# Decayed attention of a two-block network on one Trainium2 core: six gate groups go between the heads, the norm factors reach the features in one fp32r product, the sums of squares go into column groups

## The chip, the cores and the metric

The kernel runs on one core of a Trainium2 chip. Five engines of the core work side by side, each through its own list of instructions in order: TensorE (PE in the rows; PEld is its weight load), VectorE (DVE), ScalarE (ACT), GpSimd (POOL) and SyncE (SP), which issues the loads. Products go to PSUM; VectorE and ScalarE read it from there, GpSimd doesn't. The metric is the device time of one execution in microseconds.

## The reference, cut to what matters

The network is a first block (two layers of attention and a mixture of experts) and a second block of four layers: Fox (decayed attention), GLA, GDN, and Fox again, each followed by a SwiGLU. There are 256 tokens of 1024 features; the second block puts 16 meta tokens ahead of them. The change lies in the Fox layers alone:

```
def fox_mixer(h, w_in, b_f, q_gain, k_gain, w_out):
    proj = h @ w_in
    q, k, v, gate, f = jnp.split(proj, [D_MODEL, 2 * D_MODEL, 3 * D_MODEL, 4 * D_MODEL], axis=-1)
    q = rmsnorm(q.reshape(B, L, H, Dh), q_gain) * (Dh ** -0.5)
    k = rmsnorm(k.reshape(B, L, H, Dh), k_gain)
    v = v.reshape(B, L, H, Dh)
    log_f = jax.nn.log_sigmoid((f + b_f).astype(jnp.float32))
    c = jnp.cumsum(log_f, axis=1).transpose(0, 2, 1)
    ...
    # per query: softmax over earlier keys of q.k + c_query - c_key, times v
    o = o * jax.nn.sigmoid(gate)
    return (o @ w_out).astype(h.dtype)
```

H is 16 heads of Dh = 64 features. The queries of the meta tokens see meta keys only.

## The kernel before

Activations stand with features on the partitions: 8 tiles of 128 features by T2 = 272 tokens (256 in the outputs of the last layer). A projection (`proj`, L1832) makes one tile of 128 output features at a time, a group: 24 products of 128x128 weights with 128x272 activations into one PSUM tile `ps_mm`. There are 24 for 8 tiles of inputs, since weights and activations are split into a high and a low part (`wh`, `wl`; `hh`, `hl`) of the type fp32r, and high by high, high by low and low by high are summed. The pieces of the weights come through the class `Stream`: SyncE loads them ahead into `wraw`, ScalarE copies the high part (L312), VectorE subtracts for the low part (L322); of a plan whose mode is "both", GpSimd subtracts for every second piece.

The code is written in the order in which each engine's list is to stand; there is no scheduler. After a group `step` issues small work: what `later` has put into `due` for that tick, and up to `bg` = 2 pieces of `after_group` (one less when something was due). `flush` issues all that is left.

A Fox layer goes: 8 groups of queries, a small projection for log f, 8 groups of keys, 8 of values, 8 of gates, `flush`, the attention, and the output projection. Small work stands between the groups:

- `qk_evac`: ScalarE copies a group (L1977) and squares it (L1979); TensorE then sums the squares of each head by a product with `headsel` (L1974, 16 rows of output), one product after each group, 16 in a layer.
- `root`, `factor`: from these sums the factors of the norm, one row per head, on VectorE and ScalarE.
- `unit`/`one`: TensorE spreads the factors over the features by a product with `hb` (L2026, fp32, 16 rows deep), once per tile of queries or keys, 16 in a layer; VectorE multiplies (L2030) into `qS` and `kS`, with two `ps_t` tiles in turn.
- `v_tr`: TensorE transposes a tile of values (L2048, L2049), ScalarE copies it.
- `meta_scores`, `meta_soft`, `meta_norm`, `meta_trans`: the attention of the 16 meta tokens, all heads at once, in the first Fox layer alone (`lo` = 0). They come between gate groups.

The attention is a software pipeline over 16 heads (`pipe`, L701): in turn i it issues `trans` of head i-4 (TensorE transposes the weights P, L2158 and L2160; ScalarE and VectorE copy them, L2161, L2164, L2166), `scores` of head i (L2132 to L2136), `soft` of i-1 (VectorE's maxima L2142, ScalarE's exponentials L2144), `norm` of i-2 (L2149, L2151 on VectorE and GpSimd) and, every second turn, `pv` of a pair of heads (L2175 to L2182). The last five turns have no scores.

Of the kernel before, what the change touches and what calls it, by code (L numbers as in the profile page):

```python
# [26 lines left out]
# columns of the key tiles of the first mixer: first block, meta tokens, padding, both blocks  # L27
BIG = 4096.0
CAP = 128
YROWS = 14 * 128      # rows of the experts whose results go through memory; a row of zeros follows  # L30
# [4 lines left out]
# ------------------------------------------------------------------ host layout  # L35
# [95 lines left out]
def gla_masks():  # L131
# [5 lines left out]
    out[:, 0, :] = out[:, 4:].sum(1)        # the blocks of 16 and more together  # L137
# [42 lines left out]
def fm(t):  # L180
    """[tokens, 1024] to [128, 8, tokens]"""
    return np.ascontiguousarray(t.T.reshape(8, 128, -1).transpose(1, 0, 2))


def pack_rows(w, k0, n0):
    """chunks of k0 k-tiles by n0 columns: [chunk, 128, k0 * n0]"""
# [83 lines left out]
# ------------------------------------------------------------------ program  # L270

class Stream:
    """the weights, in pieces of up to 1024 columns, in the order of use: loads run ahead, and so do the splits"""
# [12 lines left out]
    def lend(self, tiles, name):  # L286
        """more room, each tile for one piece, from the first piece of that name on"""
        self.spare.extend(tiles)
        self.taker = next(i for i, p in enumerate(self.plan) if p[0][0][0] == name)

    def hold(self, name=None):
        """no loads beyond the first piece of that name, or no such bound"""
# [32 lines left out]
    def _fetch(self):  # L325
        """loads as far ahead as there are buffers that nothing to come reads"""
# [10 lines left out]
    def _reach(self, n):  # L337
        """the end of the next n pieces, not counting raw ones between them"""
# [26 lines left out]
class Net:  # L365
# [3 lines left out]
    def __init__(self, tc, aps, voff, coff, stack, phases):  # L369
# [12 lines left out]
        self.after_group = deque()      # background work for the tensor engine  # L382
        self.due = deque()              # work that waits for the evacuation of a group
        self.tick = 0
        self.bg = 2                     # pieces of background work after a group
# [4 lines left out]
    # ---- small helpers  # L390
# [40 lines left out]
    def step(self):  # L431
        """after the products of a group of a projection"""
# [8 lines left out]
    # ---- set-up  # L441
# [25 lines left out]
    # ================================================== first block  # L467
# [9 lines left out]
    def block1_alloc(self):  # L477
# [3 lines left out]
        # columns 0 .. 31 are for the router, the last two hold the conditions  # L481
# [17 lines left out]
    def mod_work(self, l, g):  # L499
        """closures: one part of the modulation of layer l, 2048 columns"""  # L500
# [2652 lines left out]
```

## Time and profile before

| what | value |
|---|---|
| three runs | 2823.67, 2824.31, 2826.16 us (median 2824.31) |
| span of the profiled execution | 2826.5 us |
| TensorE busy | 2699.9 us, 96% |
| VectorE busy | 1882.4 us, 67% |
| ScalarE busy | 1503.5 us, 53% |
| GpSimd busy | 509.4 us, 18% |
| mean granted TensorE clock | 0.977 |

The profile gives no other time of its own execution than the span, from the first to the last instruction; it is 0.3 us above the slowest of the three runs. Busy shares are averages over stages with different limits. The first Fox layer lies at about 1254 to 1444 us of the span, the second at about 2460 to 2635 us.

### The profile page before, as it was taken

Reading aid. Unit: us, or ns where it says so; the run is one execution under the profiler, and the core shown is the slowest. Engines: PE = TensorE matmul, PEld = TensorE weight load, DVE = VectorE, ACT = ScalarE, POOL = GpSimd, SP = SyncE. Lnnn points to the kernel's source line nnn. Section 1 sums busy time; section 2 is a strip of 40 time slices with the busy share of each in tenths; the row PEclk is TensorE's granted clock in tenths of the full one; section 3 lists DMA queues with packets and bytes.
Section 4 is the critical chain, followed back from the end, with each engine's and each line's share of the span. In section 5 each row is a group of like instructions: output and inputs, shape, how many; then the busy total and the mean of one; then the engine's idle time right before and its main releaser. Section 6 shows DMA issues by size and latency. Waiting matters only on the chain.

```text
span 2826.5 us, 46780 instructions
## 1 busy us (share of the span) xinstructions
PE 2699.9 (96%) x17848; PEld 2349.1 (83%) x17848; DVE 1882.4 (67%) x3094; ACT 1503.5 (53%) x2438; POOL 509.4 (18%) x482
## 2 busy tenths in 40 slices
PE   7999899999798999979899999999999999999999
PEld 4755678887576788868799998999889999987999
DVE  3257667778546889966766666665785666566664
ACT  2255467777445777754544444544553444445543
POOL 0111343231411100030210044101440200302100
PEclk9999999999799999989999999999999999999999
DMA  7544158999374699943245453455531354531554
GB/s 287 165 149 142 52 198 314 335 321 331 117 244 170 243 337 353 358 146 122 68 150 172 153 177 98 157 166 162 170 104 55 102 173 152 185 123 61 179 173 142
DMA packets 155450, 516.31 MB, mean 183 GB/s; under 512 B 22362, under 2 KB 25658, under 8 KB 155084
## 3 DMA queue, kind: packets, MB, share of 16 engines
q1 hardware_dynamic: 151440, 500.23, 52.3%
q10 hardware_dynamic: 2628, 8.83, 0.8%
q0 software_dynamic: 1152, 4.19, 0.4%
q8 instruction: 143, 2.34, 0.3%
q14 instruction: 87, 0.71, 0.1%
HBM read 504.42 MB, written 8.76 MB: 182 GB/s over the span
## 4 chain that ended last, share of the span: by engine, by line
PE 47%; DVE 6%; ACT 2%; issue 1%; POOL 1%; DMA 0%; ACTq 0%; DVEq 0%; POOLq 0%
PE ps_mm L1807 41%; DVE f L2551 1%; PE ps_t L2026 1%; DVE wl L322 1%; PE ps_s L1974 1%; DVE st L2142 1%; DVE B L2164 0%; ACT B L2144 0%; PE ps_t L2831 0%; PE ps_s L2840 0%; POOL acc L1761 0%; PE ps_mm L1860 0%; PE ps_s L2300 0%; PE ps_s L2175 0%; PE ps_o L1793 0%
## 5 line engine op out<-in xcount | busy, mean ns | idle before, releaser
L1807 PE MATMUL ps_mm<-B,wh 128*128 128x272 f32 (+1 forms) x6656 | 1271.1, 291 | 8.4 <-ACT B L1750 4.1
L322 DVE TENSOR_TENSOR wl<-wraw,wh 128x1024 fp32r<-128x1024 f32 (+2 forms) x853 | 997.8, 1196 | 128.9 <-ACT wh L312 120.1
L1807 PEld LDWEIGHTS ps_mm<-B,wh 128*128 128x128 f32 x6656 | 1049.7, 190 | 33.1 <-issue 20.2
L312 ACT ACTIVATE wh<-wraw 128x1024 fp32r<-128x1024 f32 (+2 forms) x882 | 881.7, 1013 | 197.8 <-PE ps_mm L1807 103.4
L1807 PE MATMUL ps_mm<-B,wl 128*128 128x272 f32 (+1 forms) x3328 | 962.9, 289 | 2.4 <-DVE wl L322 2.3
L1807 PEld LDWEIGHTS ps_mm<-B,wl 128*128 128x128 f32 x3328 | 631.2, 190 | 3.1 <-DVE wl L322 3.1
L1807 PE MATMUL ps_mm<-W,wh 128*128 128x512 f32 (+1 forms) x736 | 206.0, 367 | 5.2 <-ACT W L554 3.1
L1761 POOL TENSOR_TENSOR acc<-acc,sq 128x272 f32<-128x272 f32 (+1 forms) x49 | 78.8, 1608 | 641.5 <-issue 444.4
L1807 PEld LDWEIGHTS ps_mm<-W,wh 128*128 128x128 f32 x736 | 130.9, 192 | 39.3 <-ACT W L803 4.2
L1267 PE MATMUL ps_mm<-wh,W 128*128 128x512 f32 x512 | 162.1, 398 | 0.0
L1267 PE MATMUL ps_mm<-wh,XX 128*128 128x512 f32 x512 | 161.2, 396 | 0.0
L1807 PE MATMUL ps_mm<-W,wl 128*128 128x512 f32 (+1 forms) x368 | 132.0, 359 | 0.4 <-DVE wl L322 0.4
L1892 ACT ACTIVATE B<-f 128x272 fp32r<-128x272 f32 (+1 forms) x88 | 37.7, 428 | 171.1 <-DVE f L1890 171.1
L1267 PEld LDWEIGHTS ps_mm<-wh,W 128*128 128x128 f32 x512 | 96.9, 189 | 21.8
L1267 PEld LDWEIGHTS ps_mm<-wh,XX 128*128 128x128 f32 x512 | 96.7, 189 | 21.5
L1888 DVE TENSOR_TENSOR f<-ps_mm,R 128x272 f32<-128x272 f32 (+1 forms) x88 | 38.4, 437 | 112.8 <-PE ps_mm L1807 112.8
L1205 POOL TENSOR_SCALAR PP<-moec,rt_slm 128x128 fp32r<-128x128 f32 x60 | 80.7, 1362 | 177.3 <-PE ps_t L1233 177.3
L1299 PE MATMUL ps_s<-wl,ah 128*128 128x512 f32 x256 | 102.2, 399 | 5.4 <-PEq L1487 3.2
L1267 PE MATMUL ps_mm<-wl,W 128*128 128x512 f32 x256 | 103.7, 405 | 2.2 <-DVE wl L322 2.2
L1267 PE MATMUL ps_mm<-wl,XX 128*128 128x512 f32 x256 | 103.6, 405 | 1.3 <-ACT wh L312 0.9
L1299 PE MATMUL ps_s<-wh,al 128*128 128x512 f32 x256 | 101.1, 395 | 0.2 <-DVE al L1288 0.2
L1299 PE MATMUL ps_s<-wh,ah 128*128 128x512 f32 x256 | 101.2, 395 | 0.0
(727 smaller groups left out, 3653.1 us busy)
## 6 DMA issues: line engine op xcount, KB each, us to landing
wraw<-in_moe SPq DMA_DIRECT2D x376, 512.0 KB, 6.1
wraw<-in_wgu SPq DMA_DIRECT2D x176, 512.0 KB, 4.6
wraw<-in_w_mod SPq DMA_DIRECT2D x80, 512.0 KB, 4.7
wraw<-in_fox_in SPq DMA_DIRECT2D x64, 512.0 KB, 4.8
wraw<-in_wdn SPq DMA_DIRECT2D x64, 384.0 KB, 3.1
wraw<-in_wdn SPq DMA_DIRECT2D x64, 320.0 KB, 3.5
wraw<-in_gdn_in SPq DMA_DIRECT2D x32, 512.0 KB, 3.6
wraw<-in_gla_in SPq DMA_DIRECT2D x24, 512.0 KB, 3.9
```

The source lines that it names most:

```text
L312: nc.scalar.activation(wh[:, :n], t[:, :n], AF.Copy)
L322: (nc.gpsimd if pool or mode == "both" and key[1] else nc.vector).tensor_tensor(wl[:, :n], t[:, :n], wh[:, :n], op=OP.subtract)
L1205: eng.tensor_scalar(PP[:, b, i * 128:(i + 1) * 128], iota_n, u3(slm)[:, b, 2 * pair + i:2 * pair + i + 1], None, op0=OP.is_equal)
L1267: nc.tensor.matmul(ps, A[:, k, sl], B[:, d], start=n_ == 0, stop=n_ == 23)
L1299: nc.tensor.matmul(acc[c], A[:, sl], B[:, d], start=first and n_ == 0, stop=last and n_ == 11)
L1761: eng.tensor_add(self.acc[:, :n], self.acc[:, :n], sq[:, :n])
L1807: nc.tensor.matmul(ps[:, :n], A[:, k, :], B[:, :n], start=start and i == 0, stop=stop and i == tot - 1)
L1888: nc.vector.tensor_mul(t2[:, :n], pu[:, :n], self.R[:, :n])
L1892: nc.scalar.activation(ah[q][:, r, :n], av[:, :n], AF.Copy)
L1974: nc.tensor.matmul(sums[which][:16, :T2], hs[:, m, :], sq, start=m == 0, stop=m == 7)
L2026: nc.tensor.matmul(pb[:, :T2], hb[:, m * 128:(m + 1) * 128], rr[which], start=True, stop=True)
L2142: V.tensor_reduce(s[:, i:i + 1], p[:, c0:c0 + n], axis=AX.X, op=OP.max, negate=True)
```

## The change

Three things change in the Fox layers; elsewhere only comments go and line numbers shift.

1. **Sums of squares.** `add` waits for four groups and then issues four products that write to rows 0, 32, 64 and 96 of one PSUM tile, where each group had its own product before. `root` adds the four parts: six small operations on VectorE before the square root, where there were two.
2. **Factors.** They are split into a high and a low part of type fp32r in one tile `zf` (rows 0 to 15 and 32 to 47). The product in `one` is then an fp32r product 48 rows deep, not an fp32 product 16 rows deep. `hb` moves into four tiles of other buffers and is filled by 12 operations on GpSimd. During the groups of values `bg` is 3.
3. **Gates.** Only two groups of gates stand ahead of the attention. The other six are cut into halves of 12 products, and the pipeline issues one half at the end of each of its first 12 turns. Four of the eight low parts of the gates' weights go to GpSimd (mode "both"). The sigmoid becomes a tanh on ScalarE and an added 1 on GpSimd, and the values carry the factor 0.5. The copy of the meta weights (L2166) goes from VectorE to GpSimd. `yh` and `yl` get buffers of their own, since the groups of gates still read `hh` and `hl`. `meta_scores` and what follows it are issued after the two groups, with nothing of a projection between them.

```diff
+        p[12:] = [x[:3] + ("both",) + x[4:] for x in p[12:]]
...
+        sums, rr, fr = {}, {}, {}
...
+        hb = [self.t(nm, [128, 276], F32R, bufs=2)[:48, :256] for nm in ("f2", "f3") for _ in range(2)]
...
-            nc.gpsimd.tensor_copy(hb.rearrange("p (h f) -> p h f", h=16), sel[:16, :, None].to_broadcast([16, 16, 64]))
+            for i in range(4):
+                nc.gpsimd.tensor_scalar(hb[i], self.ones[:48, 0:1].to_broadcast([48, 256]), 0.0, None, op0=OP.mult)
+                for r in (0, 32):
+                    nc.gpsimd.tensor_scalar(hb[i][r:r + 16].rearrange("p (h f) -> p h f", h=4),
+                                            sel[r:r + 16, 4 * i:4 * i + 4, None].to_broadcast([16, 4, 64]), 1.0, None, op0=OP.mult)
 
         def qk_evac(which, raw):
-            def add(m, sq):
-                if m == 0:
+            sqs = []
+
+            def add(m):
+                if m == 3:
                     sums[which] = self.ps("s")
-                nc.tensor.matmul(sums[which][:16, :T2], hs[:, m, :], sq, start=m == 0, stop=m == 7)
+                for i in range(4):
+                    nc.tensor.matmul(sums[which][32 * i:32 * i + 16, :T2], hs[:, m - 3 + i, :], sqs[m - 3 + i], start=m == 3, stop=m == 7)
...
-                self.later(lambda: add(m, sq), 1)
+                sqs.append(sq)
+                if m % 4 == 3:
+                    self.later(lambda: add(m), 1)
...
         def root(which):
             R = self.R[:16]
-            t = rr[which] = self.u("zr", [16, T2], F32, bufs=2)
-            V.tensor_mul(t, R, R)
-            V.tensor_mul(t, sums[which][:16, :T2], t)
+            p = sums[which]
+            t = rr[which] = self.u("zr", [16, T2], F32)
+            V.tensor_copy(t, p[0:16, :T2])
+            for i in range(1, 4):
+                V.tensor_add(t, t, p[32 * i:32 * i + 16, :T2])
+            for _ in range(2):
+                V.tensor_mul(t, t, R)
             nc.scalar.activation(t, t, AF.Sqrt, bias=self.eps6[:16], scale=1.0 / 64)
 
         def factor(which):
             t = rr[which]
             V.reciprocal(t, t)
             V.scalar_tensor_tensor(t, t, 0.125 if which == "q" else 1.0, self.R[:16], op0=OP.mult, op1=OP.mult)
+            f = fr[which] = self.u("zf", [48, T2], F32R)
+            nc.gpsimd.tensor_scalar(f, self.ones[:48, 0:1].to_broadcast([48, T2]), 0.0, None, op0=OP.mult)
+            nc.scalar.activation(f[0:16], t, AF.Copy)
+            V.tensor_sub(f[32:48], t, f[0:16])
...
-                nc.tensor.matmul(pb[:, :T2], hb[:, m * 128:(m + 1) * 128], rr[which], start=True, stop=True)
+                nc.tensor.matmul(pb[:, :T2], hb[m // 2][:, m % 2 * 128:m % 2 * 128 + 128], fr[which], start=True, stop=True)
...
+            nc.scalar.activation(Vt[:, :, c], p[:, :256].rearrange("p (b c) -> p b c", b=2), AF.Copy, scale=0.5)
...
+        bg, self.bg = self.bg, 3
         self.proj(key, 8, T2, v_evac, c0=8)
-        sg = kraw
+        self.bg = bg
...
-            V.tensor_mul(g, ps[:, :T2], self.R)
-            nc.scalar.activation(sg[:, m, :], g, AF.Sigmoid)
-            if m == 2:
-                self.after_group.append(scratch)
-                if not lo:
-                    self.after_group.append(meta_scores)
-
-        # the attention's scratch, in the place of the raw queries and values
+            V.tensor_mul(g, ps[:, :T2], R)
+
+            nc.scalar.activation(g, g, AF.Tanh, scale=0.5)
+            nc.gpsimd.tensor_scalar(sg[:, m, :], g, 1.0, None, op0=OP.add)
...
-        self.proj(key, 8, T2, g_evac, c0=12)
+
+        self.after_group.append(scratch)
+        if not lo:
+            self.after_group.append(meta_scores)
+        self.proj(key, 2, T2, g_evac, c0=12)
         self.flush()
-        yh, yl = self.B(F32R), self.B(F32R)
-        blocks = ((16, 16, 0, 144), (144, 0, 160, 272))      # queries, keys, columns: 0 .. 143; 256 .. 271, 0 .. 255
+        hh, hl = self.hh, self.hl
+        yh, yl = (self.u(nm, [128, 8, T2], F32R) for nm in ("yh", "yl"))
+
+        def gates_left():
+            for m in range(2, 8):
+                wh, wl = (w.rearrange("p (k c) -> p k c", k=8) for w in self.ws.next((key, 12 + m // 2), m % 2))
+                p = self.ps("mm")
+                for k in (0, 4):
+                    self.group(p, wh[:, k:k + 4], wl[:, k:k + 4], hh, hl, 4, T2, k0=k, start=k == 0, stop=k == 4)
+                    if k == 0:
+                        yield
+                self.step()
+                g_evac(m, p)
+                yield
+
+        left = gates_left()
...
-                V.tensor_copy(PT[h % 4][0:16, 0:16], mm["t"][:, h * 16:(h + 1) * 16])
+                nc.gpsimd.tensor_copy(PT[h % 4][0:16, 0:16], mm["t"][:, h * 16:(h + 1) * 16])
...
-        self.pipe(16, (4, trans), (0, scores), (1, soft), (2, norm), (5, pv))
+        self.pipe(16, (4, trans), (0, scores), (1, soft), (2, norm), (5, pv), (0, lambda h: next(left, None)))
```

On TensorE, in the groups of queries of the first Fox layer, this stood before (`ps_s` takes the sums, `sq` are the squares):

```order
L1974 MATMUL ps_s_11704<-sq_11668,csts 16x272
L1974 MATMUL ps_s_11704<-sq_11671,csts 16x272
L1807 MATMUL ps_mm_11717<-B_11486,wh_11574 128x272
...
L1807 MATMUL ps_mm_11717<-B_11486,wl_11619 128x272
L1974 MATMUL ps_s_11704<-sq_11709,csts 16x272
L1807 MATMUL ps_mm_11752<-B_11486,wh_11617 128x272
...
L1974 MATMUL ps_s_11704<-sq_11744,csts 16x272
```

and now:

```order
L1807 MATMUL ps_mm_11727<-B_11486,wl_11622 128x272
L1983 MATMUL ps_s_11752<-sq_11679,csts 16x272
L1983 MATMUL ps_s_11752<-sq_11682,csts 16x272
L1983 MATMUL ps_s_11752<-sq_11685,csts 16x272
L1983 MATMUL ps_s_11752<-sq_11719,csts 16x272
L1807 MATMUL ps_mm_11766<-B_11486,wh_11620 128x272
...
L1807 MATMUL ps_mm_11766<-B_11486,wl_11689 128x272
L1807 MATMUL ps_mm_11800<-B_11486,wh_11687 128x272
```

The product that stood after every group is gone; after every fourth group four products into one `ps_s` stand in a row.

On TensorE, at the beginning of the attention of the first Fox layer, this stood before (L2119 is `meta_trans`, L1807 a gate group, L2132 to L2136 the scores of a head, L2158 the transposes):

```order
L2119 MATMUL ps_t_12856<-csts,mm_p_12781 16x16 x16
L1807 MATMUL ps_mm_12884<-B_11486,wh_12748 128x272
...
L1807 MATMUL ps_mm_12884<-B_11486,wl_12789 128x272
L2132 MATMUL ps_mm_12914<-kS_1316_11534,B_11532 128x144
L2132 MATMUL ps_mm_12914<-kS_1316_11534,B_11532 128x272
L2136 MATMUL ps_mm_12914<-causal,identb 128x16
L2132 MATMUL ps_mm_12920<-kS_1317_11535,B_11533 128x144
...
L2158 MATMUL ps_t_12959<-csts,B_11538 128x128 x3
```

and now (L2112 is `meta_scores`, L2138 `meta_trans`, L2170 to L2174 the scores):

```order
L2112 MATMUL ps_s_12690<-kS_1317_11535,B_11533 16x16
L2138 MATMUL ps_t_12721<-csts,mm_p_12714 16x16 x16
L2170 MATMUL ps_mm_12742<-kS_1316_11534,B_11532 128x144
L2170 MATMUL ps_mm_12742<-kS_1316_11534,B_11532 128x272
L2174 MATMUL ps_mm_12742<-causal,identb 128x16
L1807 MATMUL ps_mm_12754<-B_11486,wh_12556 128x272
...
L1807 MATMUL ps_mm_12754<-B_11486,wl_12609 128x272
L2170 MATMUL ps_mm_12767<-kS_1317_11535,B_11533 128x144
...
L1807 MATMUL ps_mm_12754<-B_11486,wh_12556 128x272
```

Half a group of 12 products now stands behind the scores of each of the first 12 heads, and `meta_trans` follows `meta_scores` directly.

On GpSimd, in the same stretch, this stood before (L2080 to L2084 clear scratch, L2151 normalises the weights of a head):

```order
L1968 COPY hb_11539<-csts 16x1024
L2081 MEMSET B_11530 128x512
L2084 MEMSET B_11538 128x16 x4
L2151 TENSOR_SCALAR B_11538<-B_11538,st_12926 128x272
L2151 TENSOR_SCALAR B_11538<-B_11538,st_12937 128x272
L2151 TENSOR_SCALAR B_11538<-B_11538,st_12951 128x272
```

and now (L2088 adds the 1 to a gate, L2189 is the old L2151, L322 the low part of a piece of weights, L2204 the copy of meta weights):

```order
L2088 TENSOR_SCALAR B_11531<-f_1408_12708 128x272
L2088 TENSOR_SCALAR B_11531<-f_1420_12790 128x272
L2189 TENSOR_SCALAR B_11538<-B_11538,st_12773 128x272
L322 TENSOR_TENSOR wl_12810<-wraw_12362,wh_12748 128x1024
L2189 TENSOR_SCALAR B_11538<-B_11538,st_12800 128x272
L2088 TENSOR_SCALAR B_11531<-f_1426_12853 128x272
L2204 COPY B_11530<-PmT_12738 16x16
L2189 TENSOR_SCALAR B_11538<-B_11538,st_12833 128x272
L2204 COPY B_11530<-PmT_12738 16x16
```

The normalisation of a head now stands in one queue with gates, weights and copies.

## Rows read from the trace of the kernel before

**Rows 1.** The page's first line, and the chain of waits by engine.
```profile
span 2826.5 us, 46780 instructions
...
PE 47%; DVE 6%; ACT 2%; issue 1%; POOL 1%; DMA 0%; ACTq 0%; DVEq 0%; POOLq 0%
```

**Rows 2.** Chain of waits, queries of the first Fox layer: start, us, what.
```profile
1258.10 1.48 PE ps_s L1974 x6
1259.57 3.21 PE ps_mm L1807 x24
1262.79 0.56 PE ps_s L1974 x2
```

**Rows 3.** The same chain, values and gates of the first Fox layer.
```profile
1347.49 0.22 PE ps_s L2048 x2
1347.70 0.11 PE ps_s L2049
1347.81 0.65 PE ps_t L2026 x2
1348.46 3.22 PE ps_mm L1807 x24
1351.69 1.11 PE ps_t L2026 x4
```

**Rows 4.** Windows, both attentions: busy PE, PEld, DVE, ACT, POOL; then TensorE clock, DMA.
```profile
1373.95:1418.29 44.34, 36.20 (x274) 24.83 (x272) 33.99 (x127) 25.17 (x89) 15.90 (x16) 1.00 0.02 5
2569.70:2611.16 41.46, 37.00 (x274) 25.48 (x272) 30.10 (x111) 25.30 (x89) 15.90 (x16) 0.96 0.04 13
```

**Rows 5.** Timeline of TensorE, router of the first block: start, us, what.
```profile
318.56 1.07 PE L1034 MATMUL ps_o<-W,wr 128*32 128x512 f32 x8
319.56 0.73 PE L1807 MATMUL ps_mm<-W,wh 128*128 128x512 f32 x2
```

**Rows 6.** Timeline of VectorE, and windows of tile mm_p (PE, PEld, DVE, ACT), meta attention.
```profile
1361.41 0.41 DVE L2102 TENSOR_REDUCE mm_mx<-ps_s 16x16 f32<-16x256 f32 x1
1366.16 0.24 DVE L2112 RECIPROCAL mm_s<-mm_s 16x16 f32<-16x16 f32 x1
...
1361.00:1374.00 13.00, 0.55 (x16) 0.44 (x16) 1.23 (x3) 0.42 (x1) 1.00 0.56 186
```

**Rows 7.** VectorE's groups, 1225 to 1475 us: count, busy us, mean ns, idle.
```profile
L322 DVE TENSOR_TENSOR wl<-wraw,wh 128x1024 fp32r<-128x1024 f32 (+1 forms) x51 | 61.5, 1211 | 13.2 <-ACT wh L312 10.4 <-DMA wraw<-in_fox_in 2.7
...
L2030 DVE SCALAR_TENSOR_TENSOR kS<-B,vecs,ps_t 64x256 f32<-64x256 f32 (+1 forms) x32 | 10.1, 353 | 7.7 <-PE ps_t L2026 7.6
...
L2166 DVE COPY B<-PmT 16x16 f32<-16x16 f32 x16 | 3.9, 242 | 0.5
...
L2055 DVE TENSOR_TENSOR B<-ps_mm,R 128x272 f32<-128x272 f32 x8 | 3.5, 442 | 0.1
```

**Rows 8.** Timeline of TensorE, first attention.
```profile
1383.02 0.41 PE L2132 MATMUL ps_mm<-kS,B 128*128 128x144 f32 x2
...
1383.99 0.90 PE L2175 MATMUL ps_s<-B,B 128*64 128x272 f32 x8
...
1385.25 0.55 PE L2158 MATMUL ps_t<-csts,B 128*128 128x128 f32 x3
...
1385.74 0.41 PE L2132 MATMUL ps_mm<-kS,B 128*128 128x144 f32 x2
...
1405.85 0.41 PE L2132 MATMUL ps_mm<-kS,B 128*128 128x144 f32 x2
```

**Rows 9.** Timeline of VectorE and GpSimd, first attention.
```profile
1380.52 0.16 DVE L2166 COPY B<-PmT 16x16 f32<-16x16 f32 x1
...
1381.52 1.06 POOL L2151 TENSOR_SCALAR B<-B,st 128x272 f32<-128x272 f32 x1 [1.36 <-DVE st L2149]
...
1382.27 0.34 DVE L2166 COPY B<-PmT 16x16 f32<-16x16 f32 x1
```

**Rows 10.** GpSimd's groups, whole span: count, busy us, mean ns, idle.
```profile
L322 POOL TENSOR_TENSOR wl<-wraw,wh 128x1024 fp32r<-128x1024 f32 x29 | 70.5, 2433 | 103.9 <-ACT wh L312 85.8 <-PE ps_t L2624 6.9 <-issue 6.2
```

More of the change, by code (lines that the diff above doesn't have):

```diff
@@ L1953, in fox @@
         vraw = self.B()
-        sums, rr = {}, {}
+        sums, rr, fr = {}, {}, {}
+        hb = [self.t(nm, [128, 276], F32R, bufs=2)[:48, :256] for nm in ("f2", "f3") for _ in range(2)]
         hs = self.cst("headsel").rearrange("p (m h) -> p m h", m=8)
         sel = self.cst("sel")
-        hb = self.u("hb", [16, 1024], F32)
         half = [slice(0, 64), slice(64, 128)]
@@ L2049, in v_tr @@
             nc.tensor.transpose(p[:48, 256:384], vraw[:, m, 224:272], self.ident)
-            nc.scalar.activation(Vt[:, :, c], p[:, :256].rearrange("p (b c) -> p b c", b=2), AF.Copy)
-            nc.scalar.activation(Vx[0:16, c], p[0:16, 128:256], AF.Copy)
-            nc.scalar.activation(Vx[32:48, c], p[32:48, 256:384], AF.Copy)
+            nc.scalar.activation(Vt[:, :, c], p[:, :256].rearrange("p (b c) -> p b c", b=2), AF.Copy, scale=0.5)
+            nc.scalar.activation(Vx[0:16, c], p[0:16, 128:256], AF.Copy, scale=0.5)
+            nc.scalar.activation(Vx[32:48, c], p[32:48, 256:384], AF.Copy, scale=0.5)
         def v_evac(m, ps):
@@ L2058, in fox @@
         unit("k", kraw, self.vec(f"fox_kg{j}"), kS)
+        bg, self.bg = self.bg, 3
         self.proj(key, 8, T2, v_evac, c0=8)
-        sg = kraw
+        self.bg = bg
+        sg, R = kraw, self.R
         def g_evac(m, ps):
             g = self.t("f1", [128, 276], F32, bufs=2)[:, :T2]
-            V.tensor_mul(g, ps[:, :T2], self.R)
-            nc.scalar.activation(sg[:, m, :], g, AF.Sigmoid)
-            if m == 2:
-                self.after_group.append(scratch)
-                if not lo:
-                    self.after_group.append(meta_scores)
+            V.tensor_mul(g, ps[:, :T2], R)
+            nc.scalar.activation(g, g, AF.Tanh, scale=0.5)
+            nc.gpsimd.tensor_scalar(sg[:, m, :], g, 1.0, None, op0=OP.add)
         W1, W2 = (t.rearrange("p m t -> p (m t)") for t in (qraw, vraw))
```

## The prediction

> **What bounds the kernel now.** I read the page first. Its chain of waits runs mostly over TensorE, and every other engine has a small share [rows 1]. The reader is to see from it that a product taken out of a projection shortens the kernel by its whole time, unless the engine that feeds or empties it becomes late. The same chain in order of time then gives prices. In the projections it goes from product to product without a gap: a group takes 3.22 us, and the small products between the groups stand on the chain with their full time [rows 2, 3]. Last come the attentions. They last 44.34 and 41.46 us, VectorE is busy for 33.99 and 30.10 us of them, and TensorE's busy time there, 36.20 and 37.00 us, overstates its work, since overlapping ends are modelled [rows 4]. There the chain changes engine from step to step, and TensorE waits.
>
> All prices are of one execution whose span is 2826.5 us. Its profile shows no time around the span. The span is 2.2 us over the median of the three runs, 2824.3 us, so I take the saving in microseconds off the median. A change of 0.2%, 5.6 us, is about what this measurement tells from none.
>
> **Sums of squares.** A layer has 16 products with the heads' selector. The first three take 1.48 us together, and 13 pieces of 0.56 us follow: 8.76 us [rows 2]. Now there are four bundles of four that write to different quarters of the rows. The trace has the same form elsewhere: four products of 512 columns with 32 rows of output (eight records, two to a product) took 1.00 us from the first start to the next product's start [rows 5]. Scaled to 272 columns that is 0.53 us; one alone is 0.56. I take 0.60, since loading weights doesn't shrink with the columns. Ends: 0.53, and 1.96 (four times a third of 1.48) if the four follow one another. A layer saves 8.76 - 2.40 = 6.4 us (ends 6.6 and 0.9), two layers **12.8 us**. The six operations in `root` for two, and the splitting of the factors (some 0.43 us each on VectorE), cost nothing on the path while one group and more, 3.22 us each, lie between `factor` and the first product that reads it. Uncovered, they would cost some 2.5 us in each of four places.
>
> **Factors.** A layer has 16 products with `hb`: 14 of 0.65 us and a pair of 1.11, 10.2 us [rows 3]. In fp32r the nearest row is a product of a projection, as wide and deeper: 3.22 / 24 = 0.134 us [rows 3]. Ends are that and 0.65 (no gain). I take 0.20, near the fp32r end, with some time for the change of weights. A layer saves 10.2 - 3.2 = 7.0, two layers **14.0 us** (ends 16.2 and 0). Filling `hb` on GpSimd lies beside the first groups of keys.
>
> **Three pieces of background work with the values.** The key factors now come two to a group. VectorE then has per group eight multiplications (32 in 10.1 us, so 2.5), a low part of 1.21 and a tile of values of 0.44, 4.2 us in all [rows 7]. TensorE has 3.22 + 0.33 for transposes [rows 3] + 0.40 = 3.95 us. So VectorE falls behind by some 0.3 us in each of four groups, and `one` waits for its two PSUM tiles, as `v_tr` does for its values. I take 1.5 us a layer, **-3.0 us** (ends 0 and, with the mean of 0.353 us for a multiplication [rows 7], 2.1 a layer). What is late next is the last keys, and two groups of gates still cover them.
>
> **Gates between the heads.** Before, attention and six groups took 44.3 + 6 x 3.22 = 63.7 us in the first layer [rows 3, 4]. TensorE's work is 0.97 us for the scores of a head (1383.02 to 1383.99), 1.26 for `pv` of a pair, and 0.49 for `trans` [rows 8]: 16 x 0.97 + 8 x 1.26 + 16 x 0.49 = 33.4 us, with the gates 52.7. A head takes 2.51 us now (1385.74 to 1405.85, eight heads [rows 8]), against 2.09 of work, so a turn with half a group has 3.70 us of products and should be bound by TensorE. VectorE's 34.0 us lose the copies, 3.9, and gain six gates of 0.44 and four low parts of 1.21: 37.6 us [rows 4, 7], far below. What stays are the waits after the last scores, 1405.85 to 1418.29 less 6.7 us of work, 5.7 us, and 0.42 us in each of four heads without gates, 1.7. Together 60.1 us, a saving of 3.6. In the second layer the waits are 41.5 - 33.4 = 8.1 us where the first has 10.9; in proportion 2.7. Sum **6.3 us**. Ends: all waits but the last 5.7 filled, 9.3; or none, 0. The table load for the exponential at the head of the attention, which the tanh may spare, lies among those waits.
>
> The copies that go to GpSimd have another side. One took 0.16 us alone and 0.34 while GpSimd's 1.06 us ran, and it ended with it, at 1382.61 against 1382.58 [rows 9]. Such copies leave VectorE, so by this row the sum gains a little, and I count nothing. The Trainium skill (SBUF — State Buffer, section "SBUF: two separate sides") says that VectorE and GpSimd share a pair of ports as a lock: an instruction of VectorE with two inputs in SBUF, or in its two-port mode, and one of GpSimd exclude each other to the end. This pair of rows agrees with it. By that rule 28 instructions a layer (16 normalisations, eight subtractions, four low parts) could wait up to 1.06 us each, 29.7 us; VectorE would come to 67.3 us a layer where I have 60.1, and the sum would be 12.9 us, not 27.3.
>
> **Meta tokens, first layer.** `meta_trans` now follows `meta_scores` with no group between. TensorE waits for five operations of VectorE and one of ScalarE: 0.41 + 0.24 + 1.23 + 0.42 = 2.30 us [rows 6], and six handovers of some 0.1. I take **-2.8 us**. With a table load it would be about 4. Behind the waiting transposes stand the first scores, for which VectorE and ScalarE wait.
>
> **Sum.** 12.8 + 14.0 - 3.0 + 6.3 - 2.8 = 27.3 us: 2824.3 - 27.3 = **2797 us**.
>
> **Rivals.**
> - *The four sums follow one another.* TensorE would gain 0.9 us a layer instead of 6.4; the sum is 16.3, 2808 us. Against it stands the router's row, four products in less than the time of two [rows 5]. Chance 0.12.
> - *The spread factors cost as much in fp32r*, for instance because a lone product waits for its weights: 13.3 us saved, 2811. Against it: the projection's products change weights every time, at 0.134 us [rows 3]. Chance 0.05.
> - *GpSimd and VectorE take turns in the attention, and the kernel gets slower.* GpSimd's 15.9 us gain six gates of 1.06, two low parts of 2.43 and, in the first layer, 16 copies of some 0.24 (VectorE's duration): 31.1 and 27.2 us [rows 4, 7, 9, 10]. If all of it were added to VectorE's 37.6 and 37.5 us, and the chain's other time stayed (10.3 and 11.4), the stages would take 79.0 and 76.1 us where I have 60.1 and 58.1: 36.9 more, 2834 us. It decides from 13.7 us more a layer on. For it: the waiting copy [rows 9]. Against it: most of VectorE's work there reads PSUM, the weights' normalisation was used two turns later, and 22 us of VectorE's time are free. The lock that the Trainium skill (SBUF — State Buffer, the same section) describes would be its cause. Chance 0.14, from a part to the whole: 0.04 of it still faster, 0.05 within 0.2%, 0.05 slower.
> - *Everything overlaps better*: factors at 0.134, no waits with the values, 9.3 us in the attention, 2.3 for the meta tokens: 36.5 us, 2788, or 2786 if the second attention's clock of 0.96 [rows 4] goes to 1.00. Chance 0.05.
>
> **Numbers.** My forecast has 0.62, with a range of its own from 2787 to 2807. A remainder of 0.02 goes to no case; I count half of it as no change and half as slower. Faster by over 0.2% (under 2818.7 us): 0.62 + 0.12 + 0.05 + 0.04 + 0.05 = 0.88; within: 0.06; slower: 0.06. The range reaches from the better case to a little over the two rivals of 2808 and 2811: 2784 to 2814.
>
> **What the new profile should show.** Four sums in one piece of about 0.6 us in the chain, four times a layer. The products with the factors at 0.13 to 0.25 us. TensorE waiting 1 to 2 us for `ps_t` or values in the last four groups of values. From the first scores to the output projection about 60 and 58 us, with TensorE almost without waits in the first 12 turns and VectorE at some 60%. One gap of about 3 us ahead of `meta_trans` in the first layer. The prediction is wrong if a bundle takes 1.5 us or more, if the turns with gates take clearly over 3.9 us with TensorE waiting for GpSimd's normalisation or for a PSUM tile, or if a second gap opens where the factors of queries or keys come late.

## The result and the profile after

The changed kernel took 2791.51 us (median of four runs, 2790.72 to 2799.53), the kernel before 2824.48 us in the same comparison (four runs). The ratio of the two is 0.9883, 95% interval 0.9868 to 0.9899: 33.0 us less where 27.3 were forecast.

The page of after, its first line and the chain by engine, has the shares of before [rows 1] but for ScalarE's, 1% where it was 2%:

```profile
span 2790.1 us, 46751 instructions
...
PE 47%; DVE 6%; ACT 1%; issue 1%; POOL 1%; DMA 0%; ACTq 0%; DVEq 0%; POOLq 0%
```

The gain is found by stage. A stage goes from the start of one group of products to the start of another in TensorE's timeline: *queries and keys* (Q/K) from the first group behind the norm of the tokens to the first group of values, *values* (V) to the first group of gates, *gates and attention* (G+A) to the output projection. Of each kernel (the later ones are those of the experiments) one profiled execution, in us:

| kernel | Q/K 1st | Q/K 2nd | V 1st | V 2nd | G+A 1st | G+A 2nd | ratio to before (95%) |
|---|---|---|---|---|---|---|---|
| before | 55.56 | 58.86 | 33.83 | 33.83 | 74.02 | 69.18 | 1 |
| after | 46.91 | 49.91 | 31.28 | 31.28 | 70.37 | 63.26 | 0.9883 (0.9868 to 0.9899) |
| sums_rows | 54.82 | 56.31 | 32.66 | 32.66 | 74.92 | 67.85 | 0.9977 (0.9962 to 0.9991) |
| sums_cols | 50.76 | 52.23 | 31.31 | 31.32 | 75.82 | 67.76 | 0.9932 (0.9913 to 0.9951) |
| sums_wide | 52.61 | 55.59 | 33.73 | 33.74 | 75.03 | 69.14 | 0.9983 (0.9970 to 0.9996) |
| factors | 55.74 | 57.53 | 31.75 | 31.76 | 72.99 | 66.40 | 0.9958 (0.9942 to 0.9974) |
| gates | 55.57 | 58.86 | 33.83 | 33.85 | 74.75 | 66.28 | 0.9993 (0.9981 to 1.0004) |
| no_gates | 46.90 | 49.90 | 30.31 | 30.32 | 71.11 | 64.82 | 0.9884 (0.9861 to 0.9908) |
| meta_late | 46.90 | 49.90 | 31.26 | 31.29 | 66.59 | 63.23 | 0.9868 (0.9848 to 0.9889) |
| no_both | 46.90 | 49.90 | 30.31 | 30.34 | 68.24 | 61.75 | 0.9872 (0.9852 to 0.9892) |
| bg2 | 48.41 | 49.90 | 29.65 | 29.66 | 74.59 | 65.95 | 0.9901 (0.9881 to 0.9921) |
| thirds | 48.41 | 49.90 | 31.28 | 31.42 | 66.48 | 64.57 | 0.9867 (0.9845 to 0.9890) |
| best | 48.43 | 49.90 | 30.34 | 30.34 | 64.37 | 61.73 | 0.9848 (0.9829 to 0.9867) |

Equal stages repeat to some 0.2 us where the granted clock is the same. In the first Q/K of sums_rows, sums_cols, factors, bg2, thirds and best it is 0.50 in the first groups (in best from about 1255.5 to 1258.5 us), which costs 1.5 us. In G+A such stretches at half clock come at the end of the first attention (sums_rows, sums_cols, sums_wide, gates, meta_late) or of the second (before, sums_wide): with the same attention code the first takes 44.43 us in before, without one, and 45.3, 45.4 and 46.2 us in sums_rows, sums_wide and sums_cols. They come and go with the execution; that an edit brought one is not shown, so differences of 1 to 2 us in a G+A are read with the clock beside them.

After is shorter by 17.60 us in Q/K, 5.10 in V and 9.57 in G+A: 32.3 in all. So the gain lies where it was looked for. The two spans differ by 4.1 us more, in code that the change doesn't touch; that part is not explained. The chain of waits of after, queries and keys of the first layer (start, us, what), answers to [rows 2, 3]:

```profile
1252.96 6.32 PE ps_mm L1807 x48
1259.28 0.58 PE ps_s L1983 x8
1259.87 9.27 PE ps_mm L1807 x72
1269.13 3.01 PE ps_mm L1860 x24
...
1288.62 0.32 PE ps_t L2045
1288.94 3.22 PE ps_mm L1807 x24
1292.16 0.44 PE ps_t L2045 x2
```

A bundle of sums takes 0.58 us; a factor product 0.32 alone and 0.44 for two. The third line shows what the forecast lacked: three groups in an unbroken row take 9.27 us. The first of them, behind the bundle, has the 3.22 us that a group behind a factor still takes; that leaves 3.02 for each of the others, and 3.22 is the price that I gave to all. The chain of before had such rows too, among the gates of the first layer (three groups) and of the second (five), and I didn't weigh them:

```profile
1360.98 9.27 PE ps_mm L1807 x72
...
2554.38 15.32 PE ps_mm L1807 x120
```

In the attentions, the windows of both (columns as in [rows 4]; 44.34 and 41.46 us there, without the six groups):

```profile
1342.10:1401.52 59.42, 56.59 (x419) 45.84 (x417) 38.86 (x120) 32.81 (x100) 29.34 (x40) 0.95 0.19 62
2517.85:2574.59 56.74, 53.55 (x418) 43.40 (x416) 41.91 (x121) 33.36 (x101) 31.75 (x27) 1.00 0.22 70
```

The forecast was 60.1 and 58.1. VectorE is busy for 38.9 and 41.9 us, not 37.6. The clock of 0.95 in the first row has a place. TensorE's timeline and the windows of after, meta tokens of the first layer (busy PE, PEld, DVE, ACT, POOL, then the clock):

```profile
1341.59 0.58 PE L2138 MATMUL ps_t<-csts,mm_p 16*16 16x16 f32 x16 [2.65 <-DVE mm_p L2132]
1342.10 0.85 PE L2170 MATMUL ps_mm<-kS,B 128*128 128x144 f32 x2
```
```profile
1338.00:1340.00 2.00, 0.93 (x33) 0.83 (x32) 1.14 (x3) 0.92 (x3) 2.00 (x2) 1.00 0.09 35
1340.00:1342.00 2.00, 0.41 (x16) 0.44 (x16) 1.62 (x4) 0.28 (x1) 1.59 (x2) 0.74 0.28 35
1342.00:1344.00 2.00, 2.00 (x14) 1.44 (x10) 0.58 (x1) 1.32 (x2) 0.00 (x0) 0.50 0.78 250
...
1346.00:1348.00 2.00, 2.00 (x10) 1.87 (x10) 0.00 (x0) 0.00 (x0) 0.00 (x0) 0.55 0.08 33
1348.00:1350.00 2.00, 2.00 (x18) 1.87 (x17) 0.00 (x0) 0.00 (x0) 0.00 (x0) 1.00 0.04 8
```

TensorE waits for 2.65 us (forecast 2.8), and then runs at half clock (1.2 GHz) for some 6 us. The scores of the first two heads with the half group between them take 6.13 us (1342.10 to 1348.23); in the second layer the same products take 3.37 (2517.85 to 2521.22). So the meta tokens cost 2.65 + 2.76 = 5.4 us in this execution.

### The profile page after: what moved, and what is told of

It is laid out like the page before. It is cut to its first block, busy times and chain, and to the rows that moved or that the text cites. A ratio compares the mean times of both kernels' runs of the same rounds, so it can differ in the third digit from the quotient of the medians.

```text
span 2790.1 us, 46751 instructions
## 1 busy us (share of the span) xinstructions
PE 2667.6 (96%) x17816; PEld 2341.1 (84%) x17816; DVE 1888.0 (68%) x3090; ACT 1501.4 (54%) x2438; POOL 574.3 (21%) x548
## 4 chain that ended last, share of the span: by engine, by line
PE 47%; DVE 6%; ACT 1%; issue 1%; POOL 1%; DMA 0%; ACTq 0%; DVEq 0%; POOLq 0%
PE ps_mm L1807 40%; DVE f L2589 2%; DVE wl L322 1%; PE ps_mm L2170 1%; PE ps_s L2213 1%; DVE kS L2049 0%; PE ps_t L2869 0%; PE ps_s L2878 0%; POOL acc L1761 0%; PE ps_mm L1860 0%; PE ps_s L2338 0%; DVE st L2180 0%; PE ps_o L1793 0%; DVE yl L2220 0%; DVE B L2602 0%
## 5 line engine op out<-in xcount | busy, mean ns | idle before, releaser
L1807 PE MATMUL ps_mm<-B,wh 128*128 128x272 f32 (+1 forms) x6400 | 1225.0, 291 | 8.3 <-ACT B L1750 4.1
L322 DVE TENSOR_TENSOR wl<-wraw,wh 128x1024 fp32r<-128x1024 f32 (+2 forms) x845 | 992.4, 1201 | 125.1 <-ACT wh L312 123.0
L1807 PEld LDWEIGHTS ps_mm<-B,wh 128*128 128x128 f32 x6400 | 1010.3, 190 | 20.5 <-ACT B L1750 4.4
L1807 PE MATMUL ps_mm<-B,wl 128*128 128x272 f32 (+1 forms) x3200 | 926.2, 289 | 2.4 <-DVE wl L322 2.3
L1807 PEld LDWEIGHTS ps_mm<-B,wl 128*128 128x128 f32 x3200 | 607.2, 190 | 3.1 <-DVE wl L322 3.1
L1807 PE MATMUL ps_mm<-W,wh 128*128 128x512 f32 (+1 forms) x736 | 206.4, 368 | 5.2 <-ACT W L554 3.1
L1807 PEld LDWEIGHTS ps_mm<-W,wh 128*128 128x128 f32 x736 | 131.2, 192 | 39.5 <-ACT W L803 4.2
L1807 PE MATMUL ps_mm<-W,wl 128*128 128x512 f32 (+1 forms) x368 | 132.2, 359 | 0.4 <-DVE wl L322 0.4
L1892 ACT ACTIVATE B<-f 128x272 fp32r<-128x272 f32 (+1 forms) x88 | 37.6, 428 | 171.2 <-DVE f L1890 171.2
L322 POOL TENSOR_TENSOR wl<-wraw,wh 128x1024 fp32r<-128x1024 f32 x37 | 89.7, 2424 | 139.6 <-ACT wh L312 128.4
```

The lines of the kernel that those rows point to most:

```text
L322: (nc.gpsimd if pool or mode == "both" and key[1] else nc.vector).tensor_tensor(wl[:, :n], t[:, :n], wh[:, :n], op=OP.subtract)
L1807: nc.tensor.matmul(ps[:, :n], A[:, k, :], B[:, :n], start=start and i == 0, stop=stop and i == tot - 1)
L1892: nc.scalar.activation(ah[q][:, r, :n], av[:, :n], AF.Copy)
```

## The experiments

**Does a break in a row of groups have a price, and which one?** My theory after the result was that a foreign product between two groups costs TensorE 0.2 us besides its own time. The edit of sums_rows and of sums_cols, against before:

```
-                self.later(lambda: add(m, sq), 1)
+                if m % 4 == 3:
+                    self.later(lambda: add(m), 1)
...
+                for k in range(m - 3, m + 1):                             # sums_rows
+                    nc.tensor.matmul(sums[which][:16, :T2], hs[:, k, :], sqs[k], start=k == 0, stop=k == 7)
...
+                for i in range(4):                                        # sums_cols
+                    nc.tensor.matmul(sums[which][32 * i:32 * i + 16, :T2], hs[:, m - 3 + i, :], sqs[m - 3 + i], ...)
```

> The kernel before with one edit: the sums of squares come in bundles of four, as in the change, but all four products of a bundle add into the same 16 rows, without column groups. Theory A: the change saved more than forecast because every break in a row of groups costs TensorE some 0.2 us besides the foreign product itself (a group takes 3.22 us after a break and 3.01 to 3.06 in an unbroken row). Then the queries and keys (first group of queries after the norm factor is known to the first group of values; before 55.63 and 58.69 us) take 53.2 and 56.3: bundles of 1.94 (-2.4), factors in pairs of 1.11 (+1.4), seven breaks fewer (-1.4); the kernel about 2818 us. Rival B, a break costs nothing in itself: 54.6 and 57.7, and 2821.

> The kernel before with the bundles of sums in column groups alone (and the six operations of root). Theory A (a break costs 0.2 us): queries and keys 49.2 and 52.2 us where before has 55.63 and 58.69, values 31.6 where before has 33.83, the kernel about 2807. Rival B (breaks cost nothing): 50.6 and 53.6, 2810. Rival C, the column groups don't overlap and a bundle takes 1.9 us as in the kernel without them: 53.2 and 56.3, 2818.

In the second layer, where no clock differs, Q/K took 56.31 and 52.23 us: both as by theory A. Without column groups a bundle takes 1.94 us, so the prediction's rival that the four follow one another is dead, and 4 us of the 6.6 per stage are the column groups' own. The chain of sums_rows, second layer:

```profile
2446.68 9.08 PE ps_mm L1807 x72
2455.76 1.94 PE ps_s L1977 x8
2457.70 9.27 PE ps_mm L1807 x72
```

Why a break costs that was still open. In the values of after, three transposes between two groups (two with 128 rows of output, one with 48) cost nothing but their own 0.33 us: from 1307.36 to 1310.72 us a group and they take 3.36, 27 products at 0.124. So the form of the product was a candidate. The edit against before:

```
-                nc.tensor.matmul(sums[which][:16, :T2], hs[:, m, :], sq, start=m == 0, stop=m == 7)
+                nc.tensor.matmul(sums[which][:, :T2], self.csts[:, o + 16 * m:o + 16 * m + 128], sq, start=m == 0, stop=m == 7)
```

> The kernel before with one edit: each product with the heads' selector has 128 columns of weights (the selector's 16 and the 112 constants behind it) and 128 rows of output, of which the first 16 are read as before; so it has the form of a group's products. Theory (a break costs 0.2 us because the array drains when the form of its products changes, as three transposes of 128 rows between two groups of values cost no more than their own 0.33 us): the ten lone sums among the queries and keys of the second layer cost 0.46 us each, not 0.76, and that stage takes 55.5 us instead of 58.86; about 5 to 6 us for the kernel. Rival, any foreign product breaks the row: 58.4 to 58.9 and no change in the time.

Q/K of the second layer took 55.59 us. The chain of sums_wide:

```profile
2475.95 3.02 PE ps_mm L1807 x24
2478.97 0.46 PE ps_s L1974 x2
2479.43 3.02 PE ps_mm L1807 x24
2482.45 0.46 PE ps_s L1974 x2
2482.91 0.65 PE ps_t L2026 x2
2483.56 3.21 PE ps_mm L1807 x24
```

The sum takes 0.46 us, not 0.56, and the group behind it 3.02, not 3.22. Eight times the output costs less, and the type of the product, fp32, is the same as before. Where a factor, 16 rows deep, follows (2482.91), the next group takes 3.21 again. So it is a product's form that makes the break, 16 rows of output or 16 deep here; which widths between 16 and 128 count no run tells. A transpose with 48 rows of output made none; the factor of after, 48 deep, did (3.22 us behind it). The Trainium skill (TensorEngine Tiling (Array Packing), section "Key Properties") says that a change of the tiling mode drains TensorE; the 0.2 us agree with it, though no row shows the drain itself. The prediction didn't weigh this rule.

**The factors alone, and the gates alone.** Parts 2 and 3 of the change, each on the kernel before (both with `bg` = 2, gates with a second `flush` ahead of the attention):

```
-                nc.tensor.matmul(pb[:, :T2], hb[:, m * 128:(m + 1) * 128], rr[which], start=True, stop=True)
+                nc.tensor.matmul(pb[:, :T2], hb[m // 2][:, m % 2 * 128:m % 2 * 128 + 128], fr[which], ...)   # factors
...
-        self.pipe(16, (4, trans), ..., (5, pv))
+        self.pipe(16, (4, trans), ..., (5, pv), (0, lambda h: next(left, None)))                             # gates
```

> The kernel before with the fp32r product of the factors alone (48 rows deep, hi and lo part), the sums and the gates as before. Theory A: a lone factor product takes 0.45 us after a transpose and 0.32 behind a sum, where the fp32 product took 0.65, so queries and keys take 54.3 and 57.4 us, values 32.2, a layer saves 3.8 us and the kernel takes about 2817. Rival, the price in the prediction (0.20 us for each): 7.0 us a layer, 2810.

> The kernel before with the gates between the heads alone (tanh, the added 1 and the copies on GpSimd too), sums and factors as before. Theory A: queries, keys and values unchanged (55.6, 58.7, 33.8 us); from the first group of gates to the output projection 73.8 and 66.7 us where before has 74.02 and 69.18, since four products with factors and the wait for the last keys stand ahead of the meta tokens and the attention; the kernel about 2821.5. In the first layer TensorE waits some 2.7 us for the meta tokens and its clock falls to half behind that. Rival: GpSimd holds VectorE up in the turns with gates so that they take 4 us or more, and the kernel takes 2830 or more.

With the factors alone the second layer's Q/K took 57.53 us, V 31.76 and G+A 66.40, 1.4 of the last because the clock stayed up at the attention's end where it fell in before: net 4.8 us, nearer to theory A's 3.8 than to 7.0. The gates alone won 2.9 us in the second layer, of which the same 1.4 are before's clock, and lost 0.7 in the first, where the clock fell twice (0.50 at 1353 to 1359 and 1411 to 1413 us), and their ratio holds 1. No turn took 4 us or more for GpSimd's sake: those with `pv` take 4.2 to 4.4 us, and TensorE waits for 0.41 us at most in one.

**The change without the gates.** All eight groups ahead of the attention, sums and factors as changed.

```
-        self.proj(key, 2, T2, g_evac, c0=12)
+        self.proj(key, 8, T2, g_evac, c0=12)
...
-        self.pipe(16, (4, trans), ..., (5, pv), (0, lambda h: next(left, None)))
+        self.pipe(16, (4, trans), ..., (5, pv))
```

> The changed kernel without its third part: all eight groups of gates ahead of the attention, sigmoid, copies and low parts on VectorE as before, the meta tokens between the groups; sums and factors as changed. Theory: queries and keys 46.9 and 49.9 us as in the changed kernel, values 30.3 as without GpSimd's low parts, from the first gates to the output projection 71.8 and 65.2 us (eight groups in an unbroken row, no factor among them); the kernel about 2793, so that the gates between the heads bring the changed kernel only 1 to 2 us. Rival, the prediction's sum (attention 6.3 us won, meta tokens 2.8 lost): 2795. Rival, most of the 33 us came from the gates: 2805 or more.

2791.66 us, the ratio of after. The stages of both layers sum to 293.4 us, those of after to 293.0. The third part, most of the change's lines, brings nothing that can be measured as it stands: it wins 0.7 and 1.6 us in G+A and gives 1.0 us back in each V.

**Where the gates' gain went.** Two edits on the changed kernel:

```
-            self.later(meta_trans, 1)
...
+                  (1, lambda h: meta_trans() if h == 0 and not lo else None))      # meta_late
...
-        p[12:] = [x[:3] + ("both",) + x[4:] for x in p[12:]]                       # no_both
```

> The changed kernel with one edit: meta_trans is issued at the end of the second turn of the heads, not straight behind meta_scores. Theory: the wait of 2.65 us for VectorE's operations goes, and with it the fall of TensorE's clock to half (granted 0.50 to 0.55 from 1342 to 1348 us), which cost another 2.6 us in the first two heads and the first half of a gate group. From the first group of gates to the output projection the first layer takes 65.1 us instead of 70.37, the second layer stays at 63.3, the kernel takes about 2786. Rival, the clock falls there for another reason: 67.7 and 2789. Rival, VectorE's seven operations for the meta tokens now delay the first heads: no gain.

> The changed kernel with the low parts of all gates' weights on VectorE (no second piece on GpSimd). Theory: GpSimd's 2.36 us hold up a VectorE operation with two inputs in SBUF (the low part yl took 2.21 us instead of 0.44 while one ran, and ended with it); without them every yl takes 0.44 us, TensorE's waits of 0.41 and 0.72 us in the turns with gates go, and from the first gates to the output projection the layers take 69.4 and 62.3 us instead of 70.37 and 63.26; the kernel about 2789.5. Rival: VectorE's two more low parts of 1.2 us in the turns make it late, and nothing is won or 1 us lost.

With meta_late the wait and the stretch at half clock are gone (granted clock 1.00 from 1335 to 1396 us), and G+A of the first layer fell by 3.78 us, between theory and rival: a wait of 0.47 us came ahead of the third head's scores, and the clock fell for 3 us at the attention's end (0.50 at 1397 to 1399), where TensorE had waited for 0.29, 0.44 and 0.73 us.

With no_both V fell by 0.97 and 0.94 us and G+A of the second layer by 1.51 (2.13 in the first, where the stretch at half clock behind the same wait of 2.65 us was shorter, some 3 us). The ratio doesn't part it from after; the stages do. That is the lock of the rival. The timelines of VectorE and GpSimd in after, values of the first layer, then the attentions:

```profile
1322.08 2.55 DVE L2049 SCALAR_TENSOR_TENSOR kS<-B,vecs,ps_t 64x256 f32<-64x256 f32 x8
1325.00 2.19 DVE L322 TENSOR_TENSOR wl<-wraw,wh 128x1024 fp32r<-128x1024 f32 x1
1323.72 2.39 POOL L322 TENSOR_TENSOR wl<-wraw,wh 128x1024 fp32r<-128x1024 f32 x1 [18.69 <-ACT wh L312]
...
1364.69 2.21 DVE L2220 TENSOR_TENSOR yl<-f,yh 128x272 fp32r<-128x272 f32 x1 [0.50 <-ACT yh L2219]
1364.23 2.36 POOL L322 TENSOR_TENSOR wl<-wraw,wh 128x1024 fp32r<-128x1024 f32 x1
...
2518.56 3.48 DVE L322 TENSOR_TENSOR wl<-wraw,wh 128x1024 fp32r<-128x1024 f32 x1
2518.54 2.42 POOL L322 TENSOR_TENSOR wl<-wraw,wh 128x1024 fp32r<-128x1024 f32 x1
2520.90 1.89 POOL L2088 TENSOR_SCALAR B<-f 128x272 f32<-128x272 f32 x1
```

The low part of a head's output, 0.44 us otherwise, starts while GpSimd's subtraction runs and ends 0.3 us behind it; a low part of weights takes 3.48 us instead of 1.2, and GpSimd's next operation, 0.9 us, waits in turn (1.89). The multiplications of the first row, which read PSUM, keep their 2.55 us for eight beside GpSimd. The Trainium skill (SBUF — State Buffer, section "SBUF: two separate sides") names this as an exclusive lock that an operation of VectorE with two inputs in SBUF needs; these rows agree. In no_both the same low part has its own time:

```profile
1357.81 0.44 DVE L2219 TENSOR_TENSOR yl<-f,yh 128x272 fp32r<-128x272 f32 x1 [0.50 <-ACT yh L2218]
```

**The third piece among the values, and the cut of the gates.**

```
-        bg, self.bg = self.bg, 3                                                   # bg2
...
-                for k in (0, 4):                                                   # thirds, with meta_late
+                for k, e in ((0, 3), (3, 6), (6, 8)):
```

> The changed kernel with two background pieces after a group of values, not three. Theory: TensorE's one wait of 0.84 us for the values goes and fewer factors stand in the values (30.2 us instead of 31.28), but three or four key factors move to the gates and to the end ahead of the meta tokens, where VectorE's multiplications aren't covered: from the first gates to the output projection 2 us more in each layer; the kernel about 2793.5. Rival, the prediction's price of the third piece (1.5 us a layer lost to VectorE): two pieces are the better, 2789 to 2790.

> The changed kernel with meta_trans in the second turn and the six groups of gates cut in thirds (9, 9, 6 products), one in each of 18 turns, the last two in turns without scores. Theory: all turns are then bound by TensorE (some 3.1 us), and of the waits after the last scores (2.3 us a layer) most are filled: 63.4 and 61.4 us from the first gates to the output projection, the kernel about 2782. Rival: a gate group holds its PSUM tile for three turns, the scores of the next head wait for its evacuation in six turns, 0.3 to 0.5 us each, and nothing is won over the kernel with meta_trans late alone (2786).

Two pieces made V 1.63 us shorter and G+A 4.2 and 2.7 longer: the third piece is right (bg2 also flushes twice ahead of the attention, and its first G+A holds the longest stretch at half clock, some 10 us from 1340). The 1.63 us are not the price of a wait alone: one wait of 0.85 us is gone, and four of the nine factor products left V for a later place. Thirds won nothing (G+A 66.48 and 64.57 against 66.59 and 63.23, where meta_late's first holds a stretch at half clock and thirds' doesn't): ahead of scores TensorE waits 0.40, 0.52 and 0.51 us in the first layer and 1.44, 0.46 and 0.47 in the second. That fits the rival, though its cause, the held tile, was only argued.

**Both edits together, and one more.** best is meta_late with no_both; lead also begins the output projection in the last turns:

```
-        first, rest = self.mixer_out(f"foxout{j}", yh, yl, l, lo, 0)
+        first, rest = self.mixer_out(f"foxout{j}", yh, yl, l, lo, 2)
...
+        self.pipe(16, ..., drain=lambda i: [next(first) for _ in range(2)])
```

> The changed kernel with meta_trans in the second turn of the heads and all low parts of the gates on VectorE, both edits together. Theory: the two savings add: from the first gates to the output projection 62.9 and 61.7 us (changed kernel 70.37 and 63.26), values 30.3 (31.28), the kernel about 2781. Rival: the clock falls at another wait of some 1.5 us instead (as at the end of the first attention when meta_trans alone was moved), 1.7 us in a layer: 2783 to 2785.

> As the kernel with both edits, and the first two groups of the output projection begin in the last five turns: six products before the other work of each turn. Theory: of the 2.2 to 2.3 us in which TensorE waits after the last scores some 1.5 are filled, less breaks of 0.2 us: 61.7 and 60.5 us from the first gates to the output projection (counted to its unbroken row, less the 3.8 us of its products that are done by then), the kernel about 2778.5. Rival: the splits of the output weights move into the last turns too and make VectorE late there: 2781 or more.

best took 2785.25 us, ratio 0.9848 (0.9829 to 0.9867), just clear of after's interval: it beats before by its time, and after by its stages (G+A 64.37 and 61.73, V 30.34), 7.9 us in all, even with 1.5 us for its first groups at half clock. Its G+A is 9.8 us shorter than that of no_gates, and neither has a stretch at half clock there: the third part is worth that much by its stages once the lock and the wait for the meta tokens are out of it, though the intervals of these two ratios overlap. lead took 2783.31 us (0.9846, 0.9824 to 0.9867), no difference from best: up to the products that follow the output projection (L1777) the second layer takes 168.11 us and 168.35 in best. The critical chain of lead shows VectorE's `wl` with 1.81 us in the first layer there, as the rival had it.

## Why the prediction was right, by its steps

Direction, range and the size of the two large terms held. The sum was 5 us short of the stages, and that is the net of terms that err both ways; that it came so near is in part luck. In us over both layers, from the stages and pieces above:

| step | forecast | measured |
|---|---|---|
| sums of squares | 12.8 | 13.0: 17.7 before, eight bundles of 0.58 after |
| factors | 14.0 | 12.9: per layer two of 0.32 and seven pairs of 0.445 |
| fewer breaks (not in the sum) | 0 | 4.5: what is left of the 32.3 |
| three pieces with the values | -3.0 | -1.9: after's V less that of no_gates |
| gates and meta tokens, in G+A | 6.3 - 2.8 = 3.5 | 2.3: G+A of no_gates less that of after |
| before's clock at the end of its second attention | 0 | 1.4: 41.55 us against 40.12 in no_gates |
| sum (rounded terms) | 27.3 | 32.3 |

- **Sums, factors.** Both right in size. Factors come in pairs, since no sum is due after most groups, which the working didn't see; a lone one takes 0.32 us, over the 0.13 to 0.25 that I named.
- **Breaks: the step that was mis-sized.** "In the projections it goes from product to product without a gap: a group takes 3.22 us" counted the 0.2 us of each break into the group. The price of a foreign product is its piece of the chain plus some 0.2 us when its form differs. sums_wide shows this directly: 3.3 us in one stage with no product fewer. The 4.5 us is a remainder, but the starts bear it out: ahead of the attentions the groups, projections and transposes of no_gates, the same products, take 4.6 us less than before's, and TensorE comes back to them from a product 16 or 48 deep or 16 rows wide 24 times in both layers, where before does so 49 times.
- **Values.** The direction held and the size was not far off by luck; the cause was another. With no piece on GpSimd three pieces a group don't hold TensorE up (V 30.3, no_gates and no_both), so the backlog of VectorE that I priced at 3.0 us cost nothing. It was GpSimd's low part that stopped VectorE's, and so `v_tr` once a layer (0.85 us).
- **Gates.** 59.4 and 56.7 us for the forecast's 60.1 and 58.1. With gates, a turn without `pv` takes 2.93 us (1355.11 to 1358.04), all TensorE's. Without the lock the heads and gates of the second layer win 3.1 us over no_gates (61.75 against 64.82), near the 2.7 of the forecast. The meta gap was right at 2.65 us, but its half clock cost as much again, so that the part's worth shrank to nothing next to the lock's cost.
- **Rivals.** The lock exists but touched few operations: V's 1.9 us and waits of TensorE of 0.41, 0.72 and 0.28 us, not the rival's 36.9. Of VectorE's operations in the attentions only the low parts have two inputs in SBUF, and only they took twice their time or more. GpSimd's were held too (a normalisation took 2.06 us for 0.98), but in the turns with gates TensorE waited for none of them.
- **Sums that don't come out.** The better case's terms add to 36.0 us, not 36.5, if the sums of squares stay at 12.8; its time of 2788 stays.

Left open: why in some executions the clock falls at the waits of an attention's end (before, gates, meta_late, and the three kernels with sums alone) and in others not (after, best); why the stretch at half clock behind one and the same wait of 2.65 us is shorter in no_both than in after; and the 4.1 us outside the stages.

## What to carry to other kernels

Price a small product between large ones by start-to-start times of an unbroken row and a broken one, not by its own piece of the chain: keep its form that of its neighbours, or bundle it. Before moving work between engines, look for VectorE operations with two inputs in SBUF that will run beside GpSimd's; a 2.4 us subtraction on the idle engine stopped the busy one. A wait of a few microseconds of TensorE can be paid twice, by itself and by the clock behind it; and a change of several parts is to be run without each, since here the largest part of the code was worth nothing as built, and 9.8 us by its stages after two edits of a few lines.

## What the runs showed of the hardware

- Between groups, a product with 128 rows of output took 0.46 us where one with 16 rows took 0.56, and the next group 3.02 us instead of 3.22; one transpose with 48 rows of output cost no such time. A product 48 deep (the factor of after) cost it: 3.22 us behind it.
- Four products in column groups took 0.58 us together, one alone 0.56, four into the same rows 1.94.
- After 2.65 us without work TensorE's granted clock was 0.50 (1.2 GHz): for some 6 us of the work behind it in after, some 3 in no_both. After waits of 0.3 to 0.7 us at the ends of attentions it fell in some executions, for some 3 us (7 in sums_cols), and in others not.
- VectorE and GpSimd excluded each other for whole instructions, both ways: 3.48 us for 1.2, and 1.89 for 0.9.
